# Linear attention with its projections dealt out between the steps: the values' columns one head later, other shares per head, and a scheduling priority for emptying the readout's bank

## The chip, the cores and the metric

The program runs on one core of one Trainium2 chip. The metric is the device time of one execution in microseconds (us), the median of several runs. PE is the matmul engine, PEld its weight loads, DVE the vector engine, ACT the scalar engine, POOL the general-purpose engine, and SP the engine whose queue issues the DMAs.

## The reference

The reference runs two layers over 1024 latent tokens and 256 context tokens of width 1024, all in float32. The change touches the second layer alone, a bidirectional gated linear attention with 8 heads of 128 columns:

```
ff, fb, v, q, og = split(u @ w_in)          # two forget gates, values, query, output gate
for gate, rev in ((ff, False), (fb, True)): # both directions
    f = lb + (1 - lb) * sigmoid(gate);  k = (1 - lb) * sigmoid(-gate)
    S_new = decay * S + k^T v               # chunk by chunk, started on the context
    o    += (q * decay) @ S + masked(q k^T with decays) @ v
y   = rmsnorm(o) * silu(og)                 # per head
out = h + gate * (y @ w_out);  final rmsnorm
```

## The kernel before

Every projection multiplies in three passes: weight and input are each split into a rounded high part and a low remainder, and a term is high by high, high by low and low by high (`mm3`, L103). A weight is loaded by one DMA of 512 KB (L89), its high part is cast by ACT (L93), and its low part is subtracted by POOL, or half by DVE and half by POOL (L94). The raw weight has two buffers, the high and low parts three pairs.

The stage works head by head, 0 to 7. PE's order is the order of the program text (`manual_schedule`). On the other engines a planner picks, each time the engine is free in its own model of time, the ready instruction of the best priority; the priority is the place in the text, and `high_priority(offset=n)` moves a block n places ahead.

Each head consists of

- `levels`: seven doubling steps. First DVE prepares the gates and keys: F (L889, L891), KK (L892), and QQ (L894); POOL adds the two key directions into KD (L900), which the first small matmuls (L905) read. In each step ACT gathers keys (L914), PE does 32 or 16 small matmuls into the bank `lv` (L919, L931, L940), and DVE multiplies KK and QQ by the decays (L945, L947) and shortens the table of decays `tot` (L951).
- `readout`: six groups of key transposes (`pk`, L969, copied out by ACT as `kt`, L971) and state matmuls (`pv`, L977, folded into ST by DVE, L987). Then, for each half of the tokens, twelve matmuls into the one bank `po` (L1007 to L1009). ACT squares it with a sum (L1014) and takes a root (L1015), DVE inverts (L1016) and scales the bank out into `on` (L1018). The second half needs the same bank. At the end the two halves are transposed (`pt`, L1024), multiplied by the gate `og` (L1026), split (L1032, L1033) and stored.

The projections of the coming heads are generators that sit in one queue, `Fill`. `fill.run(us)` takes matmuls from the head of the queue worth `us` by the plan's own price (a term of 512 columns 3*(512/2400+0.013) = 0.679 us, of 256 columns 0.359 us) and so places them in PE's order at that spot. When the queue is empty, the place stays empty. A head's places, as multiples of its `us`: 2 ahead of L905, 1 ahead of each of the seven steps, 0.5 ahead of each of the six groups and twice after them (4 in all), 1 after the first half of `po`, 2 after the second half, and 1 between the two halves of `pt`; 17 in all. `us` is 4.9 for head 0, 4.0 for heads 1 to 5, 3.0 for 6 and 7.

What is queued at head h: `og_proj(h)` (16 terms of 512, 10.9 us), `fkq_proj(h+1)` (two gates of 8 terms of 256 and 16 of 512 each, and q of 16 terms: 38.4 us; in head 7 `out_early` instead, 56 terms, 38.0 us), and in heads 0, 2 and 4 `v_proj(h//2+1)`, the values of the next two heads (two weights, 80 terms of 256, 28.7 us). `fill.finish(g)` empties the queue up to g: the values and og before `readout`, the next head's gates at the head's end.

Of the kernel before, what the change touches and what calls it, by code (L numbers as in the profile page):

```python
# [14 lines left out]
AF = mybir.ActivationFunctionType  # L15
ALU = mybir.AluOpType
# [16 lines left out]
PRI_E = 100  # L33
# [5 lines left out]
LG = ()  # L39
NPT = 5  # L40
PRI_T = 200


def custom(t, offset, dims):
# [5 lines left out]
def backbone_kernel(ctx: ExitStack, tc: tile.TileContext, a: dict, out):  # L50
    nc = tc.nc
    V, S, G, PE, SY = nc.vector, nc.scalar, nc.gpsimd, nc.tensor, nc.sync
# [21 lines left out]
    def ctile(shape, name, dt=F32):  # L74
        return const.tile(shape, dt, tag=name, name=name)
# [63 lines left out]
    eps_c = ctile([128, 1], "eps")  # L139
# [262 lines left out]
    for j in range(8):  # L402
# [4 lines left out]
                        scalar2=convb[:, j:j + 1], op0=ALU.mult, op1=ALU.add)  # L407
# [37 lines left out]
        for d in range(2):  # L445
# [7 lines left out]
            else:  # L453
# [4 lines left out]
                                     op0=ALU.mult, op1=ALU.add)  # L458
# [105 lines left out]
    class Unit:  # L564
# [53 lines left out]
        def turn(self, i):  # L618
# [6 lines left out]
            ptc = at.tile([128, 4, 128], F32, tag="pt", name="pt", bufs=NPT)  # L625
            with tc.high_priority(offset=PRI_T):
                S.copy(ptc, pt)  # L627
# [84 lines left out]
    fill = Fill()  # L712
# [132 lines left out]
    vts, fkq, ogs = {}, {}, {}  # L845

    def v_proj(g):
        wv = [load_w(a["wv1"][g, i], split=True) for i in range(2)]
        for tb in (8, 9) + tuple(range(8)):
            c, o = (2, tb * 128 - 1024) if tb >= 8 else (tb // 4, (tb % 4) * 128)  # L850
            ps = psC.tile([128, 512], F32, tag="mm", name="mm_v", bufs=4)[:, :256]
            yield from steps3(ps, [(u[c][0][:, k, o:o + 128], u[c][1][:, k, o:o + 128],
                                    wv[k // 4][0][:, (k % 4) * 256:(k % 4) * 256 + 256],
                                    wv[k // 4][1][:, (k % 4) * 256:(k % 4) * 256 + 256]) for k in range(8)], 256)
            vt = gb_.tile([128, 256], F32, tag="vt", name="vt", bufs=20)
            with tc.high_priority(offset=PRI_V):
                S.copy(vt, ps)
            vts[g, tb] = vt

    def fkq_proj(h):  # L860
        F = gl.tile([128, 2, T], F32, tag="F", name="F")
        KK = gl.tile([128, 2, T], F32, tag="KK", name="KK", bufs=2)
        ws = []

        def one(d, c):
            o, n = CHUNKS[c]
            ps = yield from gemm_steps(ws[d], c, psC, "mm", 4)
            with tc.high_priority(offset=PRI_E):
                S.activation(F[:, d, o:o + n], ps, AF.Sigmoid)
                S.activation(KK[:, d, o:o + n], ps, AF.Sigmoid, scale=-1.0)  # L870

        for d in range(2):
            ws.append(load_w(a["w1"][h, d], split=(h == 0)))
            for c in (2, 0) if h == 0 else (2, 0, 1):
                yield from one(d, c)
        if h == 0:

            for d in range(2):
                yield from one(d, 1)
        q = gb_.tile([128, NL], F32, tag="q", name="q")  # L880
        yield from silu_proj(a["w1"][h, 2], q)
        fkq[h] = F, KK, q

    def og_proj(h):
        ogs[h] = gb_.tile([128, NL], F32, tag="og", name="og")
        yield from silu_proj(a["w1"][h, 3], ogs[h])
# [65 lines left out]
            tot, nb = nt, nb // 2  # L952
        return QQ, AT, tot

    def readout(h, KK, QQ, AT, tot, fill, us):
        ve = (h % 2) * 128
        Vt = {tb: vts[h // 2, tb] for tb in range(TB)}
        og = ogs[h]

        ST = gb_.tile([128, 2, 8, 128], F32, tag="ST", name="ST")  # L960
        orders = ([8, 9] + list(range(0, 7)), [9, 8] + list(range(7, 0, -1)))
        cur = [None, None]
        kts = {}

        def turn(d, g0):
            grp = orders[d][g0:g0 + 4]
            pk = psC.tile([128, 4, 128], F32, tag="st", name="pk", bufs=2)
            for i, ch in enumerate(grp):
                PE.transpose(pk[:, i], KK[:, d, ch * 128:ch * 128 + 128], ident)  # L969
            kts[d, g0] = gb_.tile([128, 4, 128], F32, tag="kt", name="kt", bufs=2)  # L970
            S.copy(kts[d, g0][:, :len(grp)], pk[:, :len(grp)])  # L971

        def states(d, g0):
            grp = orders[d][g0:g0 + 4]
            pv = psC.tile([128, 4, 128], F32, tag="st", name="pv", bufs=2)
            for i, ch in enumerate(grp):
                PE.matmul(pv[:, i], kts[d, g0][:, i], Vt[ch][:, ve:ve + 128], start=True, stop=True)  # L977
            for i, ch in enumerate(grp):
                if g0 + i == 0:
                    cur[d] = ST[:, d, 1 if d == 0 else 6]  # L980
                    V.tensor_copy(cur[d], pv[:, i])
                    continue
                if g0 + i == 1:
                    nxt = ST[:, d, 0 if d == 0 else 7]
                else:
                    nxt = ST[:, d, ch + 1 if d == 0 else ch - 1]
                V.scalar_tensor_tensor(out=nxt, in0=cur[d], scalar=tot[:, d, ch:ch + 1], in1=pv[:, i],  # L987
                                       op0=ALU.mult, op1=ALU.add)
                cur[d] = nxt

        groups = [(d, g0) for g0 in range(0, 9, 4) for d in range(2)]
        for i, g in enumerate(groups):
            fill.run(us / 2)
            turn(*g)
            if i:
                states(*groups[i - 1])
        fill.run(us / 2)
        states(*groups[-1])
        fill.run(us / 2)

        ons = []
        for half in range(2):
            po = psC.tile([128, 4, 128], F32, tag="o", name="po", bufs=1)
            for i in range(4):
                ch = half * 4 + i
                sl = slice(ch * 128, ch * 128 + 128)
                PE.matmul(po[:, i], QQ[:, 1, sl], ST[:, 0, ch], start=True, stop=False)  # L1007
                PE.matmul(po[:, i], QQ[:, 0, sl], ST[:, 1, ch], start=False, stop=False)
                PE.matmul(po[:, i], AT[:, ch], Vt[ch][:, ve:ve + 128], start=False, stop=True)  # L1009
            ms = gb_.tile([128, 4], F32, tag="ms", name="ms", bufs=2)  # L1010
            on = gb_.tile([128, 4, 128], F32, tag="on", name="on", bufs=2)
            ons.append(on)
            for i in range(4):
                S.activation(on[:, i], po[:, i], AF.Square, accum_out=ms[:, i:i + 1])  # L1014
            S.activation(ms, ms, AF.Sqrt, scale=1.0 / 128, bias=eps_c)  # L1015
            V.reciprocal(ms, ms)  # L1016
            for i in range(4):
                V.tensor_scalar(out=on[:, i], in0=po[:, i], scalar1=ms[:, i:i + 1], scalar2=None, op0=ALU.mult)  # L1018
            fill.run((1 + half) * us)
        for half in range(2):  # L1020
            on = ons[half]
            pt = psC.tile([128, 4, 128], F32, tag="st", name="pt", bufs=2)
            for i in range(4):
                PE.transpose(pt[:, i], on[:, i], ident)  # L1024
            y = on.rearrange("p a b -> p (a b)")
            V.scalar_tensor_tensor(out=y, in0=pt.rearrange("p a b -> p (a b)"), scalar=gnw[:, 0:1],  # L1026
                                   in1=og[:, half * 512:half * 512 + 512], op0=ALU.mult, op1=ALU.mult)
            if h == 7:
                yhl = yT[half][:, 7]
            else:  # L1030
                yhl = gb_.tile([128, 2, 512], F32R, tag="yhl", name="yhl")
            S.copy(yhl[:, 0], y)  # L1032
            V.tensor_tensor(out=yhl[:, 1], in0=y, in1=yhl[:, 0].bitcast(F32), op=ALU.subtract)  # L1033
            if h < 7:
                SY.dma_start(y_d[h][half], yhl.bitcast(F32))
            if half == 0:
                fill.run(us)
# [38 lines left out]
    fill = Fill()  # L1076
    drain(fkq_proj(0))
    vp = v_proj(0)
    fill.todo.append(vp)
    for h in range(8):  # L1080
        og = og_proj(h)
        nxt = fkq_proj(h + 1) if h < 7 else out_early()
        need = [vp, og]
        fill.todo.extend([og, nxt])
        if h % 2 == 0 and h < 6:
            vp = v_proj(h // 2 + 1)
            fill.todo.append(vp)
        us = 4.9 if h == 0 else 4.0 if h < 6 else 3.0
        F, KK, q = fkq[h]
        QQ, AT, tot = levels(h, F, KK, q, fill, us)  # L1090
        for g in need:
            fill.finish(g)
        readout(h, KK, QQ, AT, tot, fill, us)
        fill.finish(nxt)
    gl_st.close()
    gb_st.close()
# [17 lines left out]
    half = [slice(0, 256), slice(256, 512)]  # L1114
# [109 lines left out]
```

## Time and profile before

| | |
|---|---|
| median of 3 runs | 1989.1 us (1985.41 to 1989.97) |
| the profiled execution: its time | 1988.59 us |
| its span, first to last instruction | 1986.7 us |
| busy: PE | 1886.1 us (95%) |
| busy: DVE, ACT, POOL | 58%, 48%, 24% |
| mean granted clock of PE | 0.984 |

The profile is of one execution. Idle time in brackets or behind a bar is the engine's, just ahead of the instruction, with what ended it behind the arrow. Busy time of PE includes the modelled end of each matmul, so a stall reads some 0.2 us shorter in it than between the starts of two matmuls. The stage of the change runs from 1180 to about 1910 us; a head is counted here from its first L905 to the next head's, so that the 2 `us` ahead of the next L905 belong to it.

### The profile page before, as it was taken

How to read it: one execution, taken by the hardware profiler on the slowest of the kernel's cores; microseconds unless marked ns; L12 is line 12 of the kernel's file. 1: busy time of each engine (PE TensorE's matmuls, PEld its weight loads, DVE VectorE, ACT ScalarE, POOL GpSimd, SP SyncE). 2: the span in 40 equal slices, each digit the busy share in tenths (PEclk: the TensorE clock that was granted, in tenths of full speed). 3: DMA queues.
4: the chain of work that ended last, by engine and by line, in shares of the span. 5: the costliest groups of instructions: out<-in, count | busy, mean ns of one | idle time of the engine just before them, and what ended most of it. 6: DMA issues, size and time to landing. Idle time of an engine off the chain costs nothing. (4 is left out here: it accounts for less than half of the span.)

```text
span 1986.7 us, 36590 instructions
## 1 busy us (share of the span) xinstructions
PE 1886.1 (95%) x15228; PEld 1605.0 (81%) x15228; DVE 1146.0 (58%) x1920; ACT 956.1 (48%) x1766; POOL 475.1 (24%) x309
## 2 busy tenths in 40 slices
PE   6989999999999999999989999999999999998987
PEld 5878888889888787887768889898888779777676
DVE  3766555564465556556534756564746664565656
ACT  4478666682156578556532443434324433343332
POOL 0133332320111024213232222121103212221342
PEclk9999999999999999999999999999999999999998
DMA  8222333323633336435453421111101101110643
GB/s 315 90 97 90 109 106 102 106 91 121 201 99 114 113 123 191 133 120 165 144 171 137 127 68 33 33 57 41 55 33 44 54 26 51 33 52 30 251 141 113
DMA packets 89461, 207.53 MB, mean 104 GB/s; under 512 B 9808, under 2 KB 38224, under 8 KB 88272
## 3 DMA queue, kind: packets, MB, share of 16 engines
q1 hardware_dynamic: 89296, 205.20, 31.5%
q8 instruction: 119, 1.95, 0.4%
q14 instruction: 46, 0.38, 0.1%
HBM read 155.36 MB, written 49.81 MB: 103 GB/s over the span
## 5 line engine op out<-in xcount | busy, mean ns | idle before, releaser
L94 POOL TENSOR_TENSOR w_lo<-w_raw,w_hi 128x1024 fp32r<-128x1024 f32 (+2 forms) x137 | 323.3, 2363 | 1086.7 <-ACT w_hi L93 1008.4
L103 PE MATMUL mm<-u_hi,w_hi 128*128 128x512 f32 (+1 forms) x1456 | 548.0, 376 | 6.7 <-DVE sga L422 3.6
L103 PE MATMUL mm<-u_lo,w_hi 128*128 128x512 f32 (+1 forms) x1456 | 527.6, 362 | 4.7 <-DVE u_lo L250 4.7
L103 PE MATMUL mm<-u_hi,w_lo 128*128 128x512 f32 (+1 forms) x1456 | 527.5, 362 | 0.0
L103 PEld LDWEIGHTS mm<-u_hi,w_hi 128*128 128x128 f32 x1456 | 276.6, 190 | 54.6 <-issue 9.1
L103 PEld LDWEIGHTS mm<-u_hi,w_lo 128*128 128x128 f32 x1456 | 276.0, 190 | 43.4
L103 PEld LDWEIGHTS mm<-u_lo,w_hi 128*128 128x128 f32 x1456 | 276.9, 190 | 41.7 <-DVE u_lo L250 6.6
L93 ACT CAST w_hi<-w_raw 128x1024 fp32r<-128x1024 f32 (+2 forms) x163 | 141.6, 884 | 218.8 <-PE mm L103 95.6
L103 PE MATMUL mmo<-y_hi,w_hi 128*128 128x512 f32 (+1 forms) x384 | 146.5, 381 | 7.6 <-DVE acc L780 7.6
L599 DVE CUSTOM_DVE_ANT_0 p<-s_ps,maskA 128x640 f32<-128x640 f32 (+2 forms) x160 | 110.3, 713 | 58.8 <-PE s_ps L594 58.7
L610 ACT ACTIVATE p<-p,nm 128x640 f32<-128x640 f32 (+2 forms) x160 | 118.7, 743 | 42.8 <-DVE nm L606 39.0
L103 PE MATMUL mmo<-y_hi,w_lo 128*128 128x512 f32 (+1 forms) x384 | 138.0, 359 | 0.0
L103 PE MATMUL mmo<-y_lo,w_hi 128*128 128x512 f32 (+1 forms) x384 | 137.6, 358 | 0.0
L627 ACT COPY pt<-t 128x512 f32<-128x512 f32 x168 | 94.8, 582 | 81.3 <-PE t L624 80.9
L103 PE MATMUL mm_v<-w_hi,u_hi 128*128 128x256 f32 x400 | 115.3, 288 | 0.0
L103 PE MATMUL mm_v<-w_lo,u_hi 128*128 128x256 f32 x400 | 113.1, 283 | 0.0
L103 PE MATMUL mm_v<-w_hi,u_lo 128*128 128x256 f32 x400 | 113.1, 283 | 0.0
L624 PE MATMUL t<-ident,p 128*128 128x128 f32 x672 | 98.4, 273 | 4.7 <-ACT pt L627 2.9
L103 PE MATMUL mm_o<-yT,w_hi 128*128 128x256 f32 (+1 forms) x384 | 93.2, 338 | 8.3 <-DMA yT<-y_d 3.2
L945 DVE TENSOR_TENSOR KK<-KK,tot 128x1280 f32<-128x1280 f32 x48 | 74.1, 1544 | 40.3 <-PE lv L931 25.2
L624 PEld LDWEIGHTS t<-ident,p 128*128 128x128 f32 x672 | 80.5, 141 | 19.7 <-ACT pt L627 4.9
L103 PEld LDWEIGHTS mmo<-y_hi,w_hi 128*128 128x128 f32 x384 | 73.8, 192 | 22.8 <-DVE acc L780 8.3
(219 smaller groups left out, 3492.3 us busy)
## 6 DMA issues: line engine op xcount, KB each, us to landing
w_raw<-w_in SPq DMA_DIRECT2D x66, 512.0 KB, 3.7
ada<-ada_w_in SPq DMA_DIRECT2D x48, 512.0 KB, 6.3
w_raw<-wo_in SPq DMA_DIRECT2D x32, 512.0 KB, 3.7
qt<-q_d SPq DMA_DIRECT2D x20, 512.0 KB, 4.8
y_d<-yhl SPq DMA_DIRECT2D x14, 512.0 KB, 2.7
yT<-y_d SPq DMA_DIRECT2D x14, 512.0 KB, 10.9
w_raw<-wo1m_in SPq DMA_DIRECT2D x12, 512.0 KB, 3.8
xin<-hT_in SPq DMA_DIRECT2D x5, 1024.0 KB, 9.0
```

The lines of the kernel that those rows point to most:

```text
L93: S.copy(hi[:, o:m], raw[:, o:m])
L94: eng.tensor_tensor(out=lo[:, o:m], in0=raw[:, o:m], in1=hi[:, o:m].bitcast(F32), op=ALU.subtract)
L103: ins = PE.matmul(ps, l, r, start=(first and i == 0), stop=(last and i == n - 1))
L599: V.tensor_tensor_reduce(out=p[:, :nk], in0=s_ps[:, c0[x]:c0[x] + nk], in1=self.msks[x], scale=1.0, scalar=NEG, op0=ALU.add, op1=ALU.max, ...
L610: S.activation(p, p, AF.Exp, scale=0.125, bias=nm[:, x:x + 1], accum_out=dn[:, x:x + 1])
L624: PE.transpose(pt[:, h], self.P[h][:, o:o + 128], ident)
L627: S.copy(ptc, pt)
L945: V.tensor_tensor(out=kv_, in0=kv_, in1=custom(tot, 1, [[2, nb // 2], [nb - 1, 2], [0, hb]]), op=ALU.mult)
```

## The change

`v_proj` for the next pair is queued one head later (in heads 1, 3 and 5, behind og and the next head's gates) and must be done before the readout of an even head alone. The shares `us` become a list per head. The place after the first half of `po` grows from 1 to 1.75 times `us`, the one after the second half shrinks from 2 to 1.25. The squares, the root, the inverse and the scaling of each half stand in `high_priority(offset=PRI_E)` (100 places). og has to be finished only before the `pt` transposes.

```
+GLA_US = (4.7, 3.7, 4.0, 3.7, 4.0, 3.7, 4.0, 3.0)
...
-    def readout(h, KK, QQ, AT, tot, fill, us):
+    def readout(h, KK, QQ, AT, tot, fill, us, og_steps):
...
-            for i in range(4):
-                S.activation(on[:, i], po[:, i], AF.Square, accum_out=ms[:, i:i + 1])
-            S.activation(ms, ms, AF.Sqrt, scale=1.0 / 128, bias=eps_c)
-            V.reciprocal(ms, ms)
-            for i in range(4):
-                V.tensor_scalar(out=on[:, i], in0=po[:, i], scalar1=ms[:, i:i + 1], scalar2=None, op0=ALU.mult)
-            fill.run((1 + half) * us)
+            with tc.high_priority(offset=PRI_E):
+                for i in range(4):
+                    S.activation(on[:, i], po[:, i], AF.Square, accum_out=ms[:, i:i + 1])
+                S.activation(ms, ms, AF.Sqrt, scale=1.0 / 128, bias=eps_c)
+                V.reciprocal(ms, ms)
+                for i in range(4):
+                    V.tensor_scalar(out=on[:, i], in0=po[:, i], scalar1=ms[:, i:i + 1], scalar2=None, op0=ALU.mult)
+            fill.run((1.75 - half / 2) * us)
+        fill.finish(og_steps)
+        og = ogs[h]
...
-        need = [vp, og]
+        need = [vp] if h % 2 == 0 else []
         fill.todo.extend([og, nxt])
-        if h % 2 == 0 and h < 6:
+        if h % 2 and h < 7:
             vp = v_proj(h // 2 + 1)
             fill.todo.append(vp)
-        us = 4.9 if h == 0 else 4.0 if h < 6 else 3.0
+        us = GLA_US[h]
...
-        readout(h, KK, QQ, AT, tot, fill, us)
+        readout(h, KK, QQ, AT, tot, fill, us, og)
         fill.finish(nxt)
```

## Rows read from the trace of the kernel before

**Rows 1.** Windows: the stage, then heads 1, 2, 3 and 6; columns in order: stretch, length, busy PE, PEld, DVE, ACT, POOL, then clock, DMA share, GB/s

```profile
1180.00:1910.00 730.00, 699.62 (x7627) 601.26 (x7625) 433.46 (x550) 270.72 (x531) 163.61 (x87) 0.99 0.18 60
...
1303.34:1396.55 93.21, 93.09 (x994) 81.06 (x993) 52.15 (x65) 37.06 (x70) 20.54 (x11) 1.00 0.15 46
1396.55:1489.10 92.55, 89.63 (x1020) 79.27 (x1019) 53.47 (x72) 31.37 (x68) 12.43 (x9) 1.00 0.11 36
1489.10:1575.09 85.99, 82.70 (x883) 68.99 (x882) 52.75 (x68) 36.38 (x66) 25.41 (x11) 0.98 0.15 44
...
1751.86:1833.67 81.81, 72.40 (x831) 60.70 (x830) 54.41 (x67) 29.12 (x60) 17.26 (x9) 0.96 0.11 33
```

**Rows 2.** Who PE's matmuls waited for, 1180 to 1910 us: total, times, longest

```profile
PE po L1007 <- DVE on L1018: 14.3, 6, 5.9
PE mm_o L103 <- DMA yT<-y_d: 3.2, 1, 3.2
PE pv L977 <- ACT kt L971: 2.9, 4, 0.7
PE lv L940 <- DVE QQ L947: 2.3, 1, 2.3
PE pk L969 <- DVE ST L987: 2.2, 2, 1.1
PE lv L919 <- DVE QQ L947: 1.7, 3, 0.9
...
PE mm_o L103 <- POOL w_lo L94: 0.6, 1, 0.6
```

**Rows 3.** Timeline of PE, second half of `po` in head 3: start, length, what

```profile
1558.12 0.49 PE L1007 MATMUL po<-ST,QQ 128*128 128x128 f32 x2 [3.21 <-DVE on L1018]
1558.44 0.39 PE L1008 MATMUL po<-ST,QQ 128*128 128x128 f32 x2
1558.67 0.39 PE L1009 MATMUL po<-vt,AT 128*128 128x128 f32 x2
...
1560.08 0.64 PE L1008 MATMUL po<-ST,QQ 128*128 128x128 f32 x2
1560.51 0.63 PE L1009 MATMUL po<-vt,AT 128*128 128x128 f32 x2
```

**Rows 4.** Timeline of DVE ahead of that stall, head 3

```profile
1550.80 1.48 DVE L951 TENSOR_TENSOR tot<-F 128x1280 f32<-128x1280 f32 x1
1552.31 4.51 DVE L951 TENSOR_TENSOR tot<-tot 128x640 f32<-128x640 f32 x6
...
1556.94 1.13 DVE L1018 TENSOR_SCALAR on<-po,ms 128x128 f32<-128x128 f32 x4
```

**Rows 5.** Windows with a lower granted clock: behind the stalls of heads 3 and 6

```profile
1559.40:1562.90 3.50, 3.50 (x17) 3.40 (x17) 0.00 (x0) 0.44 (x4) 0.00 (x0) 0.51 0.00 0
...
1812.00:1818.90 6.90, 3.73 (x17) 3.73 (x18) 4.47 (x12) 0.00 (x0) 0.00 (x0) 0.51 0.00 0
```

**Rows 6.** Timeline of all engines, first half of `po` in head 2

```profile
1460.62 0.39 PE L1009 MATMUL po<-vt,AT 128*128 128x128 f32 x2
...
1462.20 1.28 ACT L1015 ACT_TABLE_LOAD   x1
...
1463.50 0.30 ACT L1015 ACTIVATE ms<-ms,eps 128x4 f32<-128x4 f32 x1
...
1464.04 1.13 DVE L1018 TENSOR_SCALAR on<-po,ms 128x128 f32<-128x128 f32 x4
```

**Rows 7.** Lines L900 and L891, all eight heads: ns min/median/max

```profile
L900 POOL TENSOR_TENSOR KD<-KK x8: 2358/3547/3577, 1185.7 to 1808.4; 128x1024 f32<-128x1024 f32 x8
...
L891 DVE TENSOR_SCALAR F<-F x8: 1477/1478/3666, 1185.6 to 1808.2; 128x2560 f32<-128x2560 f32 x8
```

**Rows 8.** The page's costliest groups, whole run: busy, mean ns, idle before

```profile
L94 POOL TENSOR_TENSOR w_lo<-w_raw,w_hi 128x1024 fp32r<-128x1024 f32 (+2 forms) x137 | 323.3, 2363 | 1086.7 <-ACT w_hi L93 1008.4
```

**Rows 9.** The page's DMA issues, whole run: size, median us from issue to landing

```profile
w_raw<-w_in SPq DMA_DIRECT2D x66, 512.0 KB, 3.7
```

More of the change, by code (lines that the diff above doesn't have):

```diff
@@ L953, in levels @@
         return QQ, AT, tot
-    def readout(h, KK, QQ, AT, tot, fill, us):
+    def readout(h, KK, QQ, AT, tot, fill, us, og_steps):
         ve = (h % 2) * 128
         Vt = {tb: vts[h // 2, tb] for tb in range(TB)}
-        og = ogs[h]
         ST = gb_.tile([128, 2, 8, 128], F32, tag="ST", name="ST")
```

## The prediction

> **What bounds the kernel now.** I read the windows first. In the stage of the change PE is busy 699.6 of 730.0 us, while DVE, ACT and POOL are busy 433, 271 and 164 [rows 1]. PE's order is fixed in the text and its work is the same before and after, so the change can give or take only what PE stands idle, 30.4 us, and what it loses at a lower clock. Head by head the idle time is uneven: head 1 has 0.12 us (head 0 likewise), head 2 has 2.92 and head 3 has 3.29 (heads 4 and 5 repeat these two within 0.3), and head 6 has 9.41 [rows 1]; the rest is head 7's.
>
> The waits of PE say what this is [rows 2]. The largest, 14.3 us in 6 waits, is the second half of `po`, which waits until DVE has scaled the first half out of the same bank. The key transposes and state matmuls wait 2.9 + 2.2 us, all of it in heads 2 and 4, and the small matmuls of the doubling steps wait 2.3 + 1.7 us, nearly all in head 6, whose `us` is 3.0. The remaining large one, 3.2 us for `yT`, is head 7's first load.
>
> The timeline of head 3 shows how the `po` wait comes about. PE stands 3.21 us [rows 3]. DVE is inside the next head's chain of decays meanwhile: seven L951 instructions from 1550.80 to 1556.8, and only then the inverse and, at 1556.94, the four scalings, done at 1558.07 [rows 4]. After the stall the granted clock reads 0.51 for 3.5 us, that is the lower level, 1.2 GHz, for nearly all of it [rows 5], and a pair of matmuls takes 0.43 us where it took 0.23 just before [rows 3].
>
> Where DVE is free the same eviction is short. In head 2 the last matmul starts at 1460.62 and ends some 0.2 us later, and the scaling is done at 1465.17 [rows 6]: 4.3 us, against a place of 1 x 4.0 us that the fill offers. So every head with 4.0 waits a little even undisturbed, and heads 3, 5 and 6 wait long.
>
> **The change part by part.** *Shares.* With the plan's own prices I dealt out both versions by hand. Before, heads 0 to 7 place 83.3, 72.5, 68.2, 58.9, 68.2, 58.9, 49.2 and 48.9 us; after, 77.9, 63.2, 63.9, 63.2, 63.9, 63.2, 63.9 and 48.9. The sums agree (508.1), so no work is saved. In heads 3 and 5 the queue before ran dry after 2.7 of the 8.0 us behind the second half; after, it runs dry in heads 2, 4 and 6 at 4.8 of 5.0 us, so that no matmul of a projection stands between the two `pt` groups there. An odd head now queues og, gates, q and the first 13.6 us of the values, an even head the values' last 15.1, og, gates and q.
>
> *The place behind the first half* becomes 1.75 x 3.7 = 6.5, 1.75 x 4.0 = 7.0, 8.2 (head 0) or 5.25 us (head 7). An undisturbed eviction (4.3) is covered in all; one like head 3's, 4.1 us of placed work and 3.4 of stall between the starts, 7.5 us, would still wait 1.0 in an odd head and 0.5 in an even one. I book the 14.3 us as gone and 1.0 us as left, 15 at the most (six heads, each late like head 6: 5.9 + 3.4 us of cover = 9.3, less 6.8).
>
> *The priority* chooses among instructions that are ready in the planner's model. L951 stood first although it is later in the text, so it was probably ready first, and a priority doesn't change that. I give it no gain of its own; the wider place is the cover.
>
> *The clock.* Head 3's lower stretch holds some eleven pairs of matmuls at 0.43 instead of 0.23, and the first of the wide ones: about 1.7 us. Heads 3, 5 and 6 lose that each, 5.1 us, and it goes with their stalls.
>
> *Head 6* goes from 3.0 to 4.0. Its idle time besides the 5.9 of `po` is 9.41 - 5.85 = 3.5 us at the steps; heads 1 to 5 at 4.0 have none there. Booked as gone: 3.5.
>
> *Odd heads at 3.7.* Between 0 at 4.0 and 3.5 at 3.0 a straight line gives 1.05 us a head. Such waits start only once a margin is used up, so I take 0.5 in each of three heads, 1.5 in all; bounds 0 and 3.2.
>
> *The key transposes.* Heads 2 and 4 wait 2.6 us each there (5.1 in all [rows 2]) because the next head's F is complete just then and its DVE instructions, up to 3.67 us long [rows 7], stand ahead of the state updates. After the change it is the odd heads 1, 3 and 5 whose gates are complete among these groups (before the third), and the even ones get theirs complete only behind `po`. Three heads at 2.6 instead of two: +2.6. Bounds: all gone, -5.1, or twice as long in each, +10.4.
>
> *Even heads' second half.* The gates' preparation now falls behind the first half, beside KD on POOL. From the end of `po` to the second `pt` there are 5.0 us of fill and one `pt` group, some 5.3 us, for an eviction of 4.3. Bounds 0 and 4.0 us a head (9.3 - 5.3); nearest is the undisturbed one, with at times one L891 in front. I take 1.0 in each of three, +3.0.
>
> L891 takes 1.48 us in most heads and 3.67 in the worst; POOL's KD takes 2.4 to 3.6 us and follows straight behind L892, as L891 can [rows 7]. The Trainium skill (SBUF — State Buffer, Who interferes with whom) says that a DVE instruction in a two-port mode and a POOL instruction lock each other out for a whole instruction; the two sizes agree with it, and by that rule the even heads would pay this 2.2 us each, 3.6 us more than my sum.
>
> The root's table load takes 1.28 us, and the root starts 0.02 us behind it [rows 6]. The Trainium skill (ScalarE: Activation LUTs, What ACT_TABLE_LOAD costs) adds a drain of about 1.38 us to each switch; the row shows none. With it the eviction would last 5.7 us, and the sum would be 1.1 us longer.
>
> *The values' projection* moves with its two 512 KB loads on SP's queue, four half casts, four half splits, 240 matmuls and ten copies, past og's one load and the gates' and q's three. Cost taken: nothing. The cover is the loads' lead; in the whole stage PE waits once, 0.6 us, for a low part, and that in the output projection [rows 2]. og's later `finish` places nothing, since og has left the queue by the seventh step of every head.
>
> *Head 7* keeps its shares, the 3.2 us for `yT` and the clock behind it.
>
> **Sum.** -14.3 + 1.0 - 5.1 - 3.5 + 1.5 + 2.6 + 3.0 = -14.8 us. The profiled execution took 1988.6 us, 1.9 more than its span and 0.5 less than the median. 1988.6 - 14.8 = 1973.8, and with half a microsecond to the median 1974.
>
> **The rivals.** *All of it hides.* F's preparation fits between the state updates and behind the bank: -22.9 and -5.1 for the transposes, some -25 with small rests, 1961 to 1967. For it: head 1 and head 0 run now with 0.1 us idle at full load. Against: DVE must do the same preparation somewhere in each head.
>
> *The stall moves.* The odd heads wait twice as long at the transposes (+10.4) and the even ones 2.2 us at the second `pt` (+6.6): -22.9 + 1.0 + 1.5 + 10.4 + 6.6 = -3.4, about 1985. For it: what delayed `po` in head 3 was the next head's preparation, which isn't removed. The Trainium skill's rule on the shared port (SBUF — State Buffer, Who interferes with whom) speaks for this one.
>
> *The change does not reach the wait.* DVE orders itself so that the scaling comes later by as much as the place grew: 1989, within 0.2%.
>
> *Slower: the values' weights come late.* They hold two of the three pairs until their last block, now inside an even head, and only og's 10.9 us stand between that and the next gates. Were a load and its split exposed, that is 3.7 us for the DMA [rows 9], 2.4 for POOL [rows 8] and 1.7 for the clock behind such a stall: three times 7.8 = 23.4 us, 1997. It decides from 5 us in each of the three. Against it: the gates' raw weight lands while the values run, and before, the same order of weights cost no wait [rows 2].
>
> **How the numbers follow.** Chances: the forecast (1968 to 1981) 0.50, all hidden 0.20, the stall moves 0.17, no reach 0.05, slower 0.08. The range 1961 to 1986 leaves out the last two, and tails. 0.2% is 4 us, about what a measurement of this kernel can tell from no change. The case in which the stall moves lies half inside it, so faster 0.79, same 0.13, slower 0.08.
>
> **What would show it.** Right: `po <- DVE on` under 2 us in all, no stretch at the lower clock between 1540 and 1820 us, head 6 with under 2 us idle, and PE idle in the stage near 18 us. The waits at `pk` and `pv` should be in heads 1, 3 and 5 and gone from 2 and 4. Wrong: a new wait `pt <- DVE on` of over 2 us in heads 2, 4 and 6 with L891 or L951 in front of the inverse, waits on w_hi or w_lo at the first gate matmuls of heads 2, 4 and 6, or the lower clock in another place.

## The result and the profile after

The changed kernel takes 1971.85 us (median, 1970.83 to 1974.83), the kernel before beside it 1989.53 us. The ratio is 0.9916, with a 95% interval of 0.9903 to 0.9929, that is 14 to 19 us less. The profiled execution took 1970.83 us with a span of 1969.0, against 1986.7 before.

Where the 17.7 us of the span come from is read by cutting both traces at the first small matmul of head 0 and of head 7 (and once more 79 us behind the latter). The first fence is the kernel before, with the lower stretch of head 5, which [rows 5] doesn't show; the fence behind it is the one after. The columns are those of [rows 1].

```profile
0.00:1201.13 1201.13, 1147.99 (x7305) 966.00 (x7305) 680.02 (x1311) 667.65 (x1205) 293.85 (x215) 0.99 0.40 130
1201.13:1833.67 632.54, 610.34 (x6714) 528.27 (x6713) 373.36 (x474) 239.25 (x472) 132.90 (x71) 0.99 0.13 41
1736.90:1740.40 3.50, 3.50 (x19) 3.50 (x19) 0.29 (x1) 0.00 (x0) 0.00 (x0) 0.51 0.00 0
1833.67:1913.00 79.33, 70.11 (x788) 55.66 (x788) 45.38 (x64) 26.06 (x50) 23.63 (x13) 0.94 0.59 212
1913.00:1986.70 73.70, 57.64 (x426) 55.09 (x425) 47.26 (x72) 23.12 (x40) 24.75 (x10) 0.89 0.36 118
```

After, with heads 1, 2, 3 and 6 as in [rows 1], and the one stretch at a lower clock that is left in these heads:

```profile
0.00:1199.01 1199.01, 1145.45 (x7302) 964.38 (x7302) 680.98 (x1311) 667.48 (x1205) 293.70 (x215) 0.99 0.40 130
1199.01:1818.63 619.62, 605.35 (x6717) 526.28 (x6716) 360.33 (x474) 237.96 (x472) 124.93 (x71) 1.00 0.13 42
1295.13:1382.79 87.66, 85.45 (x981) 75.00 (x981) 50.37 (x71) 30.12 (x66) 12.23 (x9) 1.00 0.13 43
1382.79:1469.62 86.83, 84.23 (x921) 72.04 (x921) 52.27 (x67) 36.40 (x67) 22.70 (x11) 1.00 0.14 44
1469.62:1557.32 87.70, 85.47 (x982) 75.00 (x981) 49.78 (x69) 30.65 (x67) 12.24 (x9) 1.00 0.13 43
1629.20:1632.60 3.40, 3.40 (x18) 3.40 (x17) 3.33 (x5) 0.01 (x1) 0.00 (x0) 0.50 0.02 5
1733.38:1818.63 85.25, 82.84 (x915) 70.91 (x914) 52.08 (x66) 36.16 (x67) 22.10 (x11) 1.00 0.13 40
1818.63:1898.00 79.37, 71.44 (x801) 56.65 (x801) 45.61 (x64) 26.71 (x51) 23.58 (x13) 0.96 0.57 208
1898.00:1969.00 71.00, 54.99 (x413) 52.41 (x411) 47.21 (x71) 22.48 (x39) 24.73 (x10) 0.91 0.37 123
```

Heads 0 to 6 give 12.9 us (632.5 to 619.6). PE's idle time in them falls by 7.9 (632.54 - 610.34 = 22.2, now 14.3), and its busy time by 5.0 for the same work (6714 and 6717 recorded matmuls). Most of that is the clock: before, three stretches with 10.7 us of busy time read 0.51 (3.50 and 3.73 in [rows 5], and 3.50 in head 5), after, one of 3.40 us reads 0.50. At half the speed that is an estimated 3.7 us; the views give no cause for the other 1.3. Head 7 and all behind it give 2.7 (153.0 to 150.4), and the stretch ahead of head 0 gives 2.1, of which only 0.4 is the change's (head 0's `us` is 0.2 smaller, and twice that stands ahead of the cut). The heads are now even: 87.7, 86.8, 87.7, and head 6 has 2.4 us idle where it had 9.4.

Who PE waited for in the stage, to be laid beside [rows 2]:

```profile
PE po L1007 <- DVE on L1019: 7.6, 3, 2.6
PE pv L977 <- ACT kt L971: 4.7, 9, 0.7
PE mm_o L104 <- DMA yT<-y_d: 3.1, 7, 1.0
...
PE mm_o L104 <- POOL w_lo L95: 1.7, 2, 1.1
PE lv L920 <- DVE QQ L948: 1.5, 4, 0.6
PE pv L977 <- DVE ST L987: 1.1, 3, 0.4
```

The wait of the second half of `po` is halved, not gone, and it has moved: 2.4 to 2.6 us in each of heads 2, 4 and 6, none in the odd heads. The waits at `pk` and `pv`, formerly in heads 2 and 4, are now three times 1.9 us in heads 1, 3 and 5. The 2.3 us at a late step of head 6 are gone. There is no wait of `pt`. The lines for `yT` and `w_lo` lie in head 7 and in the output projection, into which this window reaches some 15 us further than that of [rows 2].

The timeline of head 2 shows what the new `po` wait is (all engines, from the end of the first half to the start of the second; PE's projections left out):

```profile
1443.72 0.39 PE L1009 MATMUL po<-vt,AT 128*128 128x128 f32 x2
1444.14 0.28 ACT L1015 ACTIVATE on<-po 128x128 f32<-128x128 f32 x1 [6.83 <-PE po L1009]
...
1444.66 1.05 ACT L94 CAST w_hi<-w_raw 128x1024 fp32r<-128x1024 f32 x1
1445.61 0.28 ACT L1015 ACTIVATE on<-po 128x128 f32<-128x128 f32 x1
...
1445.78 2.39 POOL L95 TENSOR_TENSOR w_lo<-w_raw,w_hi 128x1024 fp32r<-128x1024 f32 x1 [19.69 <-ACT w_hi L94]
1445.87 0.59 ACT L870 ACTIVATE F<-mm 128x512 f32<-128x512 f32 x1
...
1446.50 3.03 DVE L890 TENSOR_SCALAR F<-F,oml,lb 128x2560 f32<-128x2560 f32 x1 [6.76 <-ACT F L870]
...
1446.60 0.61 ACT L871 ACTIVATE KK<-mm 128x512 f32<-128x512 f32 x1
1447.22 1.28 ACT L1016 ACT_TABLE_LOAD   x1
...
1448.52 0.30 ACT L1016 ACTIVATE ms<-ms,eps 128x4 f32<-128x4 f32 x1
...
1449.45 1.54 DVE L893 TENSOR_SCALAR KK<-KK,oml 128x2560 f32<-128x2560 f32 x1
...
1450.91 0.17 DVE L1017 RECIPROCAL ms<-ms 128x4 f32<-128x4 f32 x1
1451.00 1.46 DVE L892 TENSOR_SCALAR F<-F 128x2560 f32<-128x2560 f32 x1
...
1452.38 1.11 DVE L1019 TENSOR_SCALAR on<-po,ms 128x128 f32<-128x128 f32 x4
...
1453.55 0.49 PE L1007 MATMUL po<-ST,QQ 128*128 128x128 f32 x2 [2.60 <-DVE on L1019]
```

The last gates of head 3 leave PE just as `po` does. On ACT a weight's cast and two gate evictions stand among the four squares or behind them (1.9 us more to the table load than in [rows 6]). On DVE the next head's L890 and L893 stand before the inverse (root done at 1448.82, inverse at 1450.91: 2.1), and L892 between the inverse and the scaling (1.3 more than where nothing stands between, as in E5 below). With the undisturbed 4.3 us of [rows 6] that makes 9.6; read in the same way, the scaling is done at 1453.49, 9.6 us after the last matmul. The place covers some 6.8, and the 2.8 left are the row's 2.60 and the 0.2 by which a stall reads short.

### The profile page after: what moved, and what is told of

Read it like the earlier page. It is cut to its first block, busy times and chain, and to the rows that moved or that the text cites. A ratio compares the mean times of both kernels' runs of the same rounds, so it can differ in the third digit from the quotient of the medians.

```text
span 1969.0 us, 36589 instructions
## 1 busy us (share of the span) xinstructions
PE 1877.2 (95%) x15228; PEld 1599.7 (81%) x15228; DVE 1134.1 (58%) x1920; ACT 954.6 (48%) x1766; POOL 467.0 (24%) x309
## 5 line engine op out<-in xcount | busy, mean ns | idle before, releaser
L95 POOL TENSOR_TENSOR w_lo<-w_raw,w_hi 128x1024 fp32r<-128x1024 f32 (+2 forms) x137 | 314.9, 2302 | 1109.3 <-ACT w_hi L94 1059.7
L946 DVE TENSOR_TENSOR KK<-KK,tot 128x1280 f32<-128x1280 f32 x48 | 80.1, 1670 | 41.0 <-PE lv L932 23.9
```

The lines of the kernel that those rows point to most:

```text
L95: eng.tensor_tensor(out=lo[:, o:m], in0=raw[:, o:m], in1=hi[:, o:m].bitcast(F32), op=ALU.subtract)
L946: V.tensor_tensor(out=kv_, in0=kv_, in1=custom(tot, 1, [[2, nb // 2], [nb - 1, 2], [0, hb]]), op=ALU.mult)
```

## Experiments

No experiment leaves out any of the work. The table has the time beside the kernel before on the same chip, and from the one trace of each the length of heads 0 to 6 (same cuts, windows view) and PE's waits in these heads (view of waits): second half of `po`, `pt`, key transposes with state matmuls, and the small matmuls of the steps. Times in us.

| kernel | median | ratio to before, 95% | heads 0 to 6 | po | pt | pk, pv | lv |
|---|---|---|---|---|---|---|---|
| before | 1989.5 | 1 | 632.5 | 12.8 | 0.2 | 5.1 | 3.4 |
| after | 1971.9 | 0.9903 to 0.9929 | 619.6 | 7.6 | 0 | 5.8 | 0.9 |
| E1 after, no priority | 1971.5 | 0.9893 to 0.9923 | 619.3 | 7.4 | 0 | 5.8 | 0.9 |
| E2 before, priority alone | 1990.0 | 0.9988 to 1.0009 | 632.9 | 12.9 | 0.5 | 5.1 | 3.7 |
| E3 before, places alone | 1982.3 | 0.9955 to 0.9978 | 629.8 | 4.9 | 6.0 | 5.1 | 3.0 |
| E4 shares and values alone | 2002.1 | 1.0047 to 1.0074 | 647.3 | 23.8 | 0 | 5.8 | 0.9 |
| E5 after, priority 400 | 1967.3 | 0.9875 to 0.9904 | 614.9 | 0 | 3.4 | 5.8 | 0.9 |
| E6 after, second bank | 1963.5 | 0.9852 to 0.9894 | 613.4 | 0 | 1.8 | 5.8 | 0.9 |
| E7 after, values early | 1988.2 | 0.9983 to 1.0003 | 639.9 | 9.9 | 2.6 | 9.2 | 1.5 |
| E8 after, old `us` | 1977.1 | 0.9926 to 0.9966 | 625.5 | 1.1 | 6.0 | 8.1 | 2.3 |
| E9 before, second bank | 1972.4 | 0.9893 to 0.9923 | 617.3 | 0 | 0.5 | 5.1 | 3.7 |
| E10 E6, places swapped | 1962.6 | 0.9846 to 0.9878 | 609.3 | 0 | 0 | 5.8 | 0.9 |
| E11 E6, two banks for pv | 1962.3 | 0.9836 to 0.9872 | 609.8 | 0 | 2.1 | 4.6 | 0.9 |
| E12 E10 and E11 | 1959.7 | 0.983 to 0.9861 | 606.2 | 0 | 0 | 4.8 | 0.9 |

**E1 and E2: does the priority do anything?** E1 takes it out of the changed kernel, E2 puts it alone into the kernel before.

```
-            with tc.high_priority(offset=PRI_E):      # E1; E2 adds this line to before
```

> The changed kernel without the priority; shares, the values' place and the places behind the halves stay. Theory (the wider place and the shares do it, the priority nothing, since DVE's order follows what is ready first): 1972 us, within 2 us of the changed kernel, with the waits for po at 7 to 9 us as there. Rival (the priority is what shortens the eviction): the first half is scaled out 1 to 3 us later in the middle heads, po waits 14 us or more, 1980 us or more.

> The kernel before with the priority alone. Theory: 1989 us, within 2 us of before, with po waiting 13 to 15 us, since the chain L951 stands ahead of the scaling because it is ready first. Rival (the priority does it): the scaling moves ahead of L951, po waits under 7 us and the lower clock behind it goes, 1977 us or less.

Neither differs: the intervals of E1 and of the whole change lie on each other, E2's holds 1, and the waits are those of the kernels that they were made from. A priority of 100 places does nothing here.

**E3 and E4: the places and the shares apart.** E3 is before with the places 1.75 and 1.25. E4 is the changed kernel with the old places 1 and 2 and without the priority.

```
-            fill.run((1 + half) * us)                 # E3
+            fill.run((1.75 - half / 2) * us)
```

> The kernel before with the places 1.75 and 1.25 behind the halves alone. Theory: the waits for po of heads 1 to 5 and 7 go (8.4 us) with the two lower stretches of the clock behind heads 3 and 5 (3.4), head 6 keeps some 3.6 of 5.9 us (9.3 less 5.25, and some clock): some 13 us less than before, 1976 us. Head 6's waits in the steps (3.5 us) and those of the key transposes in heads 2 and 4 (5.1 us) stay. Rival (the shares per head do it): within 4 us of before.

> The changed kernel with the old places 1 and 2 behind the halves and no priority: the shares per head and the values one head later alone. Theory: head 6's waits in the steps go (3.5 us), the key transposes wait in three odd heads instead of two even ones (+3.3), and the first half of heads 2, 4 and 6, which takes 9.5 us to be scaled out in the changed kernel, finds a place of 4 us: about 5 us each and the lower clock behind it, more than before. In sum 1988 to 1996 us, no gain. Rival (the even spread of the work is what gains): 1980 us or less.

E3 gains 7 us where 13 were expected (2.8 of them in heads 0 to 6), E4 loses 12.5, more than its range. The parts don't add: -7 and +12.5 apart, -17.7 together. In E3 the place taken from the second half is missed there:

```profile
PE pt L1024 <- DVE on L1018: 6.0, 2, 3.0
PE po L1007 <- DVE on L1018: 4.9, 3, 3.9
...
```

These 6.0 us are 3.0 each in heads 3 and 5, whose queue is dry behind `po`; what is left of `po`'s wait is mostly head 6's (3.9). The lower clock, which was to go from heads 3 and 5, now stands behind these `pt` waits (0.50 from 1566.7, 0.53 from 1744.0). In E4 the even heads, which now get their next gates beside `po`, wait 5.6 to 6.0 us each with the old place, and the odd ones, for which none was expected, 2.1: 23.8 in all, with a mean granted clock of 0.98 in heads 0 to 6 where it is 1.00 after. The wide place is what makes the new shares bearable, and the new shares with the later values are what gives the wide place its gain; E7 and E8 below part these two.

**E5: a priority above the cast's.** The cast of the weights stands in `high_priority(offset=PRI_W)` with 300, so at 100 a cast that stands up to 200 places further on in the text still goes first.

```
-            with tc.high_priority(offset=PRI_E):
+            with tc.high_priority(offset=PRI_W + 100):
```

> The changed kernel with the eviction moved 400 places ahead instead of 100, which is more than the 300 of the weights' casts. What is left of the po wait, 7.6 us in heads 2, 4 and 6, has on ACT a cast (1.05 us) and two gate evictions (1.2 us) between the squares and the root, and on DVE the next head's L890 and L893 ahead of the inverse. Theory (100 places were too few to pass the cast; a larger offset lets the eviction go first): po waits under 1.5 us, 1964 us. Rival 1 (a priority does nothing here, whatever its size): 1972 us. Rival 2 (the next head's preparation is only pushed behind, and the second half's scaling comes late for the pt transposes): pt waits 1.5 to 3 us in each even head, 1968 to 1972 us.

The same stretch of head 2 (last matmul pair of the first half at 1446.02):

```profile
1446.44 0.28 ACT L1015 ACTIVATE on<-po 128x128 f32<-128x128 f32 x1 [6.83 <-PE po L1009]
...
1447.46 1.06 ACT L94 CAST w_hi<-w_raw 128x1024 fp32r<-128x1024 f32 x1
1448.54 1.28 ACT L1016 ACT_TABLE_LOAD   x1
...
1450.37 1.13 DVE L1019 TENSOR_SCALAR on<-po,ms 128x128 f32<-128x128 f32 x4
...
1451.44 0.60 ACT L870 ACTIVATE F<-mm 128x512 f32<-128x512 f32 x1
...
1452.07 1.61 DVE L890 TENSOR_SCALAR F<-F,oml,lb 128x2560 f32<-128x2560 f32 x1 [0.57 <-ACT F L870]
...
1457.29 3.51 POOL L901 TENSOR_TENSOR KD<-KK 128x1024 f32<-128x1024 f32 x1 [6.30 <-DVE KK L893]
...
1458.58 2.90 DVE L952 TENSOR_TENSOR tot<-tot 128x640 f32<-128x640 f32 x1
...
1460.55 0.60 PE L1027 MATMUL pt<-ident,on 128*128 128x128 f32 x4
1461.41 0.16 DVE L1017 RECIPROCAL ms<-ms 128x4 f32<-128x4 f32 x1
```

All four squares pass the cast and the gate evictions, and the scaling is done at 1451.50, 1.6 us before the second half starts. `po`'s 7.6 us are gone. The preparation that was put off meets the second half instead: its inverse comes only at 1461.41, behind an L952 that began 0.1 us before the root was done (1458.72) and took 2.90 us beside POOL's KD; one of the same size took 0.81 in head 2 before (at 1446.32). `pt` waits 3.4 us in all. Heads 0 to 6 are 4.7 us shorter than after, between the theory and its rival.

**E6, E9 and E10: a second bank for `po`.** The second half goes into the bank that the small matmuls of the steps have left by then. E6 does it to the changed kernel, E9 to the kernel before with nothing else changed. E10 is E6 with the places behind the two halves swapped, 1.25 and 1.75.

```
-            po = psC.tile([128, 4, 128], F32, tag="o", name="po", bufs=1)
+            po = psC.tile([128, 4, 128], F32, tag=("o", "lv")[half], name="po", bufs=1)
```

> The changed kernel with the second half of po in the bank of the small matmuls (lv), which is idle in the readout: the second half no longer waits for the first half's scaling. Theory (the rest of the po wait is worth its 7.6 us and the lower clock behind it): po waits 0, 1963 to 1965 us. Rival (DVE has the same work to do ahead of the second half's scaling, and the wait moves to the pt transposes, 1.5 us in each even head): 1967 to 1969 us.

> The kernel before with the second half of po in the bank lv, nothing else. Theory (what the changed kernel gained is at bottom the one bank's wait): the 14.4 us of po waits and the 5.1 us of lower clock behind them go, some 3 us come up at the pt transposes of heads 3, 5 and 6, where the queue is nearly dry: 1970 to 1975 us, as much as the whole change. Rival (DVE's order sets the pace, and the wait moves on whole): 1982 us or more.

> The changed kernel with two banks, and the places behind the halves 1.25 and 1.75 instead of 1.75 and 1.25. Theory (with two banks the work is of more use behind the second half): the pt waits left there, 1.8 us, go, 1961 to 1962 us. Rival (no matter): as with two banks alone, 1963 to 1964 us.

All of E9's waits in heads 0 to 6:

```profile
PE pv L977 <- ACT kt L971: 2.9, 4, 0.7
PE lv L940 <- DVE QQ L947: 2.3, 1, 2.3
PE pk L969 <- DVE ST L987: 2.2, 2, 1.1
PE lv L919 <- DVE QQ L947: 1.4, 2, 0.9
PE pt L1024 <- DVE on L1018: 0.5, 2, 0.3
```

The `po` wait is gone, and hardly any comes up at `pt` (0.5). One tag gives 17.5 us, as much as the whole change. So the dependence on the one bank was what the stalls came from; the order of work on ACT and DVE only set how long they were. The 5.1 us of clock didn't go as expected: PE's busy time in these heads falls by 2.7 (610.3 to 607.6), and three stretches at the lower level are left, in other places than before, behind the transposes of heads 2 and 4 and in head 6 (0.50 from 1776.9). The first two, in the columns of [rows 1]:

```profile
1449.30:1452.70 3.40, 3.40 (x11) 2.81 (x10) 2.37 (x8) 0.00 (x0) 0.00 (x0) 0.51 0.00 0
1623.20:1626.60 3.40, 3.40 (x13) 3.01 (x13) 2.91 (x10) 0.00 (x0) 0.00 (x0) 0.52 0.00 0
```

In E6 the gain over the changed kernel is 8 us by the medians. E10 removes the 1.8 us left at `pt` and shortens heads 0 to 6 by 4.0 (the other 2.2 are busy time of PE, without a known cause), but its time can't be told from E6's.

**E7 and E8: the values' move, the shares.** E7 queues the values in the even heads again, E8 has the old `us`; all else is as changed.

```
-        if h % 2 and h < 7:                           # E7
+        if h % 2 == 0 and h < 6:
...
-        us = GLA_US[h]                                # E8
+        us = 4.9 if h == 0 else 4.0 if h < 6 else 3.0
```

> The changed kernel with the values queued in the even heads again; shares, places and priority stay. Theory (the later place of the values is what gives head 6 work behind its first half, and spreads the rest): head 6's queue runs dry ahead of the place behind its first half, so PE waits there 5 us or more with the lower clock behind it, and heads 3 and 5 run dry ahead of the pt transposes and wait 2 to 3 us each there: 1982 to 1988 us. Rival (the values' place is of no weight): 1971 to 1974 us.

> The changed kernel with the old shares (4.9, then 4.0, then 3.0 in heads 6 and 7). Theory (the shares have to match what is queued): head 6 waits in its steps (3.4 us) and at po (9.4 less a place of 5.25, about 4 us, and the clock), and heads 2 and 4 run dry ahead of the pt transposes and wait about 3.5 us each: 1980 to 1986 us. Rival (the shares of single heads are of no weight once the place behind the first half is wide): 1971 to 1975 us.

E7 loses the whole gain. Its waits in heads 0 to 6:

```profile
PE po L1007 <- DVE on L1019: 9.7, 3, 4.2
PE pk L969 <- DVE ST L987: 4.5, 3, 2.3
PE pv L977 <- ACT kt L971: 4.4, 6, 0.7
PE pt L1027 <- DVE on L1019: 2.6, 1, 2.6
...
```

Shares of one size need work of one size, and that is what the later values give. Head 6 alone waits 10.6 us at the four places; heads 3 and 5 wait at `po`, 2.7 each, and not at `pt` as expected. E7's heads 0 to 6 are 7.4 us longer than before, and yet its time is the same: all behind them is 5.8 us shorter in the profiled execution (147.2 for 153.0), where the wait for `yT` is 0.3 for 3.2 and that of `po` in head 7 (1.5) is gone. E8 is 5 us slower than the change, between the ranges of its theory and its rival: with the old shares heads 2 and 4 wait 3.0 us each at `pt`, the 4 us expected at `po` of head 6 don't come, head 6 has its waits in the steps back (2.3), and the transposes cost 8.1 in place of 5.8.

**E11 and E12: the transposes.** On top of E6's edit, `pv` alternates between the two banks of `po`, by direction, so that `pk` has the two others to itself. E12 has E10's places too.

```
-            pv = psC.tile([128, 4, 128], F32, tag="st", name="pv", bufs=2)
+            pv = psC.tile([128, 4, 128], F32, tag=("o", "lv")[d], name="pv", bufs=1)
```

> The changed kernel with two banks, and the state matmuls' pv in the banks o and lv in turn, so that pk has both st banks. Theory (the odd heads' waits of pv for the copy of a pk that was just issued, 4.7 us in nine, come from pv taking that pk's bank because the earlier pv is late to be read): they go, 1957 to 1959 us. Rival (DVE's preparation of the next head holds the state updates themselves, and pv or po waits for those): pv and po wait for DVE ST by as much, 1962 to 1964 us.

> All of these together: two banks for po, pv in o and lv, places 1.25 and 1.75. Theory: no wait for po, pt or pv over 1 us in all, 1955 to 1958 us. Rival (one of the two does nothing): 1961 us or more.

E11 in heads 0 to 6:

```profile
PE pv L977 <- DVE ST L987: 3.5, 3, 1.2
...
PE pv L977 <- ACT kt L971: 1.1, 3, 0.4
...
```

`kt`'s wait goes from 4.7 to 1.1, but the one for ST comes up from 1.1 to 3.5, once per odd head: the bank was one of two limits, and when DVE gets to fold `pv` into ST is the other. Together these waits fall by 1.2 us. Heads 0 to 6 are 3.6 us shorter than in E6; most of that is less busy time of PE (2.7), for which the views give no cause, and `pt` waits 0.3 more. E11's time (1962.3, in the rival's range) can't be told from E6's. E12 has the lowest median, 1959.7 us, 12 us less than the change; its theory that no wait of `pv` would be left was wrong by 4.8 us.

## Why the prediction came out as it did

The time was right, 1974 against 1971.9, and so was the sign. Two large terms were wrong, in opposite directions.

**`po`'s wait, -14.3 + 1.0.** Measured 7.6 us left, three times 2.4 to 2.6. The step that failed is "one like head 3's" as the worst case for most heads, and 0.5 for an even one. The bound named beside it, 15 us if every head were late like head 6, was the right case for three heads: the eviction takes 9.6 us in head 2. The prediction did say that in even heads the gates' preparation falls behind the first half, but charged it to the second half alone.

**The even heads' second half, +3.0.** Measured nothing. By then the preparation is through; F and KK were made while the first half was emptied. The charge was real and stood one place too late: E5 puts the preparation off and finds 3.4 us at `pt`.

**The key transposes, +2.6.** Moved to heads 1, 3 and 5 as said, but with 1.9 us each and not 2.6: 5.8 in place of 5.1, +0.7.

**Head 6, -3.5, and the odd heads at 3.7, +1.5.** The steps' waits go from 3.4 to 0.9 in heads 0 to 6; the 0.9 is 0.3 in each odd head where 0.5 was booked.

**The clock, -5.1.** The three stretches of heads 3, 5 and 6 went, but one at 0.50 came in head 4 (from 1629.2), behind a `po` wait that had been booked as gone. So an estimated 3.7 us went. PE's busy time fell by 5.0, which comes near to 5.1 only through another 1.3 us without a known cause. The 1.7 a head holds (half of 3.5), though the working counts eleven pairs where the trace of head 3 has six at 0.43.

**The sum.** The terms speak for heads 0 to 6 and, by 1.5 us of `po`'s wait, for head 7. There 12.9 + 1.5 = 14.4 us went, against 14.8. The errors are +6.6 at `po`, -3.0 at the second half, -1.9 at the transposes, -0.5 at the steps, +1.4 at the clock, and -2.2 for small waits and busy time that no term stands for. So the agreement to 0.4 us is largely luck. The other 3.3 us came, but for some tenths, from stretches that the change leaves alone. The part ahead of head 0 lasted from 1197.5 (E6) to 1205.7 us (E2) in these profiled executions, with the same text but for head 0's `us`, so 3 us there mean nothing.

**The priority, nothing.** Right for 100, by E1 and E2. The reason given, that L951 had been ready first, isn't the whole of it: at 400 the same block does pass the cast and the gate evictions on ACT (E5), whose own offsets are 300 and 100. For L951 itself the reason is not refuted: in E5 the second half's inverse still stands behind an L952 that had begun. 400 in the kernel before was not run.

**The values' projection, nothing.** Right in the sense that no wait for a weight came up in heads 0 to 6. As a part of the change it was worth far more than nothing: E7. Pricing each edit by itself missed that; the places, the shares and the values' move are one change in three lines.

**The rivals.** The stall did move, but from one head to another and not to the `pt` of the even heads; as a whole that case (1985) didn't come. All hidden (1961 to 1967) is what E6, E10 and E11 reach with another bank. Late weights were not seen. The signs: `po` under 2 us failed, no lower clock failed by one stretch, which is also the sign named as wrong, the lower clock in another place; head 6 under 2 us failed by 0.4; PE idle near 18 us came out at 21.0 (1180 to 1892 us), where the prediction's own terms without the clock, 30.4 - 9.7, give 20.7; the move of `pk` and `pv` held.

## What to carry to other kernels

Where one buffer is filled, emptied through two engines and filled again, look first for a buffer that is idle at that moment: here one borrowed bank was worth as much as a rearranged stage. Where a stage is fed by hand-made shares, price the edits together, since a place is worth what the queue holds when it is reached. A priority is to be read against the priorities of what stands ahead, not by itself.

## What the runs showed of the hardware

The same L890 took 3.03 us in head 2 of the changed kernel, where POOL's L95 ran until 1448.17, and 1.61 in E5, where L95 had ended a microsecond before. The Trainium skill (SBUF — State Buffer, Who interferes with whom) has a DVE instruction in a two-port mode and a POOL instruction shut each other out for whole instructions; these two numbers agree (from 1446.50 to 1448.17 and 1.61 more are 3.28 us, against 3.03), and the 1.4 us between them lay ahead of the inverse that `po` waited for.

How long a stall is does not settle whether a lower clock follows. After, `po` waited 2.4 to 2.6 us in heads 2, 4 and 6, and the granted clock fell to 0.50 for 3.4 us behind the wait of head 4 alone (from 1629.2). In E1, with the same waits (2.2 to 2.6), it fell behind that of head 2 alone (0.51 from 1456.3). In E5, E6, E10, E11 and E12, whose longest waits are 1.2 us at most, the granted clock of heads 0 to 6 is 1.00 in the windows; but in E9 it fell in heads 2 and 4 (0.51 and 0.52), whose longest wait is 1.1 us and where the kernel before, with the same waits at the transposes, reads 1.00. What decides it, these runs do not show.
